# Two-layer encoder: keys and queries of the second attention group placed by DMA, and output-weight sums formed in DRAM

## The chip, the cores and the metric

The kernel runs on one core of one Trainium2 chip. TensorE (PE) multiplies matrices out of SBUF into PSUM; VectorE (DVE), ScalarE (ACT) and GpSimd (POOL) work on tiles in SBUF and PSUM, and SyncE (SP) issues most of the DMA transfers. The metric is the device time of one execution in microseconds, and a kernel's time is the median of its runs.

## What is computed

Two encoder layers over 1024 tokens of width 1024, in float32. Layer 0 runs two groups of eight attention heads side by side: group A is dense grouped-query attention, group B is latent attention, whose keys and queries are made from compressed latents. Layer 1 is windowed attention with sixteen heads. Cut to what the change touches:

```python
def mla_attention(q_lat, q_rope, c_kv, k_rope, w_uv):          # group B of layer 0
    scale = (B_NOPE + B_ROPE) ** -0.5
    sc = (einsum('bqhc,bsc->bhqs', ql, c_kv) + einsum('bqhr,bsr->bhqs', qr, k_rope)) * scale
    p = softmax(sc, axis=-1)
    o_lat = einsum('bhqs,bsc->bqhc', p, c_kv)
    return einsum('bshc,chd->bshd', o_lat, w_uv)
...
    return concatenate([oa, ob], axis=-1) @ w_out               # both layers end in a product with w_out
```

## The kernel before

**Precision.** A float32 product is made of three fast products: each operand is split into a high part (a cast by ScalarE) and a low part (the operand less its high part, by VectorE), and `mm3` (L644) adds high by high, high by low and low by high.

**Attention in layer 0.** `run_groups` (L1185) goes over 32 steps, which the code numbers 0 to 31: a step is one head and one half of the queries, 0 to 15 for group A and 16 to 31 for group B. In a step, `softmax_unit` (L1145) makes four blocks of 128 queries by 1024 keys: scores on TensorE, the row maximum on VectorE (tile nm), the exponential on ScalarE (tile Pa in group A, Pb in group B), and the division by the row sum on GpSimd. `pv_step` (L1164) takes the blocks of the step before: TensorE transposes them, ScalarE and VectorE split the transposed block (tiles hla or hlb), and TensorE multiplies it with the values.

**Scores of group B.** For head h, `qk_of` (L1432) adds three products: q1 by k1, q2 by k2 and q1 by krl. q1 and k1 hold the high parts of the 64 plain dimensions in partitions 0 to 63 and rotary parts above them. q2 and k2 hold, in two halves of 64 partitions, high and low parts in such an order that one product gives both cross terms.

**Preparing heads.** `b_heads(p, half)` (L1399) makes these tiles for heads 2p and 2p+1 and one half of the 1024 positions. One product of 128 partitions by 512 holds the keys of both heads, another their queries. The parts are taken out of PSUM 64 partitions at a time: six casts on ScalarE, four subtractions on VectorE and two copies on GpSimd (`K2E`, L1393). Rotary parts of q1 come from the scratch tensors qr_sp in DRAM, which `b_qrope` (L1342) writes. The table B_AT (L66) puts the eight calls at steps 15, 15, 19, 19, 22, 23, 27 and 27.

**Weight sums.** The two products with w_out use a scheme with fewer block products, which needs four sums of blocks of w_out for each layer and each column half. `weight_sums` (L1460) makes them ahead of time: SP loads a block into an SBUF tile, GpSimd issues transfers that add further blocks onto it, and SP stores the tile to ws_sp in DRAM after each addition. The table WS_AT (L60) puts that at steps 19 to 26. `quarter` (L1648) loads the sums later.

**What sets the order.** No engine's program is written out. All operations are recorded with their dependencies, and `Recorder.run` (L259) simulates them on a model of the engines; the times at which they start there give the order in which they are emitted. In this model an issue on SP holds it for 450 ns, and a transfer ends 500 ns after its bytes, or 3000 ns where it adds:

```python
dma_free = max(dma_free, t + 1300) + nb / (205.0 if "accum_op" in o.call[2] else 410.0)
fin = dma_free + (3000 if "accum_op" in o.call[2] else 500)
busy[e] = t + (450 if e == "SP" else o.dur)
```

On the chip each engine then works through its own program in order. All recorded operations are issued from one line, so the profile gives them L551 and tells them apart by tile.

Of the kernel before, what the change touches and what calls it, by code (L numbers as in the profile page):

```python
# [19 lines left out]
P = 128  # L20
# [38 lines left out]
W2_ENG = ("act", "dve")  # L59
WS_AT = {19: ((0, 0, False),), 20: ((0, 0, True),), 21: ((0, 1, False),), 22: ((0, 1, True),),  # L60
         23: ((1, 0, False),), 24: ((1, 0, True),), 25: ((1, 1, False),), 26: ((1, 1, True),)}
WS_SHIFT = 0
# [52 lines left out]
class Recorder:  # L115
# [143 lines left out]
    def run(self):  # L259
# [131 lines left out]
        while started < N or ev:  # L391

            for e in engs:
# [5 lines left out]
                while h:  # L399
# [12 lines left out]
                    if e == "SP" or (o.call[0].__name__ == "dma_start"):  # L412
                        nb = 4 * max(self._region(v)[2] * max(1, self._region(v)[3])
                                     for v in list(o.call[1]) + list(o.call[2].values())
                                     if isinstance(v, VP) or hasattr(v, "tensor"))
                        dma_free = max(dma_free, t + 1300) + nb / (205.0 if "accum_op" in o.call[2] else 410.0)
                        fin = dma_free + (3000 if "accum_op" in o.call[2] else 500)
                        busy[e] = t + (450 if e == "SP" else o.dur)
                    else:
                        fin = o.end  # L420
                        busy[e] = o.end
# [152 lines left out]
def encoder_kernel(ctx: ExitStack, tc: tile.TileContext, xt, ada_t, w_c1, w_c2, w_c3, w_g0, w_uq, w_ukv, w_out0, w_v1,  # L574
# [69 lines left out]
    def mm3(ps, L, R, start, stop, **kw):  # L644
        first = mm(ps, lhsT=L[0], rhs=R[0], start=start, stop=False, **kw)
        mm(ps, lhsT=L[0], rhs=R[1], start=False, stop=False, **kw)
        mm(ps, lhsT=L[1], rhs=R[0], start=False, stop=stop, **kw)
        return first

    def rstd_of(ss, n, width):  # L650
# [748 lines left out]
    def b_heads(p, half):  # L1399
# [9 lines left out]
        mm3(ps, L, R, True, True)  # L1409
        k1 = [B["k1"][e % 3], B["k1"][o % 3]]  # L1410
        nc.scalar.copy(k1[0][0:64, c], ps[0:64, :])
        nc.scalar.copy(k2[o][64:128, c], ps[64:128, :])
        nc.scalar.copy(k1[1][0:64, c], ps[64:128, :])
        K2E(k2[e][0:64, c], f(k1[0][0:64, c]))
        sub(k2[e][64:128, c], ps[0:64, :], f(k1[0][0:64, c]))
        sub(k2[o][0:64, c], ps[64:128, :], f(k2[o][64:128, c]))
        ps = PA(f"qn{p}{half}")
        for k in range(2):
            L = [a[:, p * P:(p + 1) * P] for a in B["uq"][k]]
            R = [a[:, c] for a in B["cq"][k]]  # L1420
            mm3(ps, L, R, k == 0, k == 1)
        nc.scalar.copy(q1[e][0:64, c], ps[0:64, :])
        nc.scalar.copy(q1[o][0:64, c], ps[64:128, :])
        nc.scalar.copy(q2[e][64:128, c], ps[0:64, :])
        K2E(q2[o][0:64, c], f(q1[o][0:64, c]))
        sub(q2[e][0:64, c], ps[0:64, :], f(q1[e][0:64, c]))
        sub(q2[o][64:128, c], ps[64:128, :], f(q1[o][0:64, c]))

# [27 lines left out]

    ws_sp = {(l, a, j): dr.tile([P, 1024], F32, name=f"ws{l}{a}{j}") for l in range(2) for a in range(1, 5) for j in range(2)}
    w_out = [w_out0, w_out1]

    def weight_sums(l, j, third, mark):  # L1460

        t = U(f"ws{l}{j}{int(third)}")
        w = lambda b, k: w_out[l][b, 2 * k + j]
        load(t, w(1, 0) if not third else w(0, 0), mark)
        for a, b, k in [(3, 1, 0)] if third else [(1, 1, 1), (2, 0, 0), (4, 0, 1)]:
            nc.gpsimd.dma_start(out=t, in_=w(b, k), accum_op=ALU.add)
            nc.sync.dma_start(out=ws_sp[l, a, j], in_=t)
# [586 lines left out]
```

## Time and profile before

| | us |
|---|---|
| Median of 3 runs | 1178.45 |
| Lowest and highest run | 1177.72, 1179.77 |
| The profiled execution | 1180.8 |
| Its span, from first to last instruction | 1178.1 |
| Mean granted TensorE clock, share of full speed | 0.992 |

A row of the profile reads: line, engine, operation, tile written, tile read, shapes and count; then busy time in us and mean ns of one; then the time that the engine idled just before such instructions, and what ended that. A waiting row reads: engine and its tile, what it waited for, us in total, times, longest us. A row of transfers reads: engine whose queue issued them, count, KB each, median us from issue to landing.

These slices of the span (40 equal ones, busy tenths) show where group B lies: it is worked on from about 420 to 650 us, slices 15 to 22.

```profile
PE   7999999999999999999999999999999999999996
DVE  8974889888887988888889988959776597765885
```

### The profile page before, as it was taken

To read this page: it belongs to the slowest core of one execution; us is meant where nothing else is said; L and a number is where in the kernel's file an instruction comes from. 1 tells how busy PE (TensorE), PEld (TensorE's weight loads), DVE (VectorE), ACT (ScalarE), POOL (GpSimd) and SP (SyncE) were. 2 spreads that over 40 slices of the span, in tenths; PEclk is the share of its full clock that TensorE was granted. 3 is DMA by queue.
4 is the path that set the end of the run, shared out by engine and by line. 5 is a ranking of instruction groups with operands and counts; after the bars stand their busy time and mean duration, and the time that the engine had idled before them with its cause. 6 is when DMAs were issued, how large, how long until landed. Compare 5 with 4: busy or idle time off the path is not lost.

```text
span 1178.1 us, 17460 instructions
## 1 busy us (share of the span) xinstructions
PE 1140.4 (97%) x6070; PEld 957.6 (81%) x6070; DVE 948.4 (81%) x1678; ACT 699.9 (59%) x1406; POOL 599.9 (51%) x579
## 2 busy tenths in 40 slices
PE   7999999999999999999999999999999999999996
PEld 7898877878877878788877887988888888888885
DVE  8974889888887988888889988959776597765885
ACT  5553356565555777787778832327765365565723
POOL 1334496957854645554445444704465266445414
PEclk9999999999999999999999999999999999999998
DMA  9601433232221148786125333400002212036413
GB/s 368 253 1 66 163 117 125 90 111 89 84 63 54 52 116 222 186 217 175 37 88 225 117 143 125 161 19 8 31 18 91 72 37 90 19 144 237 139 35 143
DMA packets 41671, 133.42 MB, mean 113 GB/s; under 512 B 4592, under 2 KB 9200, under 8 KB 41584
## 3 DMA queue, kind: packets, MB, share of 16 engines
q1 hardware_dynamic: 38192, 122.88, 29.4%
q0 software_dynamic: 2304, 8.39, 4.2%
q8 instruction: 47, 0.77, 0.3%
q10 hardware_dynamic: 1088, 1.05, 0.3%
q14 instruction: 40, 0.33, 0.1%
HBM read 101.24 MB, written 31.06 MB: 112 GB/s over the span
## 4 chain that ended last, share of the span: by engine, by line
PE 77%; DVE 11%; ACT 5%; DMA 3%; issue 2%; POOL 1%; SPq 0%; POOLq 0%; ACTq 0%; DVEq 0%
PE psum L551 77%; DVE nm L551 2%; DMA ada<-in_ada_t 2%; DMA w2s<-in_w_c 1%; DMA w31s<-in_w_c 1%; ACT k L551 1%; DVE hla L551 1%; ACT Pa L551 1%; ACT q L551 1%; DVE adag L551 1%; DVE xr L551 1%; ACT Pb L551 1%; DVE hl L551 1%; DVE p L551 0%; DVE hlb L551 0%
## 5 line engine op out<-in xcount | busy, mean ns | idle before, releaser
L551 DVE TENSOR_REDUCE nm<-psum 128x1 f32<-128x1024 f32 x128 | 154.6, 1217 | 16.4 <-PE psum L551 14.7
L551 POOL TENSOR_SCALAR p<-p,dn 128x384 f32<-128x384 f32 (+1 forms) x128 | 71.8, 580 | 154.9 <-ACT p L551 74.6
L551 PE MATMUL psum<-hla,VA 128*128 128x512 f32 x256 | 94.1, 427 | 9.0 <-DVE hla L551 6.5
L551 POOL TENSOR_SCALAR Pa<-Pa,rs 128x1024 f32<-128x1024 f32 x64 | 78.9, 1238 | 43.4 <-DVE rs L551 41.3
L551 POOL TENSOR_SCALAR Pb<-Pb,rs 128x1024 f32<-128x1024 f32 x64 | 72.1, 1128 | 41.6 <-DVE rs L551 39.6
L551 ACT CAST hla<-psum 128x512 fp32r<-128x512 f32 x128 | 71.3, 596 | 36.8 <-PE psum L551 30.0
L551 PE MATMUL psum<-hlb,VB 128*128 128x512 f32 x256 | 90.9, 427 | 2.2 <-DVE hlb L551 1.5
L551 DVE TENSOR_TENSOR hla<-psum,hla 128x512 fp32r<-128x512 f32 x128 | 83.8, 681 | 11.3 <-ACT hla L551 10.9
L551 ACT ACTIVATE Pa<-psum,nm 128x1024 f32<-128x1024 f32 x64 | 71.6, 1121 | 33.6 <-DVE nm L551 28.4
L551 PE MATMUL psum<-ident,Pa 128*128 128x128 f32 x512 | 89.0, 273 | 1.0 <-DVE q L551 0.8
L551 ACT ACTIVATE Pb<-psum,nm 128x1024 f32<-128x1024 f32 x64 | 71.9, 1124 | 26.8 <-DVE nm L551 24.2
L551 DVE TENSOR_TENSOR hlb<-psum,hlb 128x512 fp32r<-128x512 f32 x128 | 81.9, 683 | 7.2 <-ACT hlb L551 5.8
L551 PE MATMUL psum<-k,q 128*128 128x512 f32 x256 | 84.3, 400 | 1.0 <-ACT Pb L551 1.0
L551 DVE CUSTOM_DVE_ANT_0 p<-psum,bias,rows_g 128x384 f32<-128x384 f32 (+1 forms) x128 | 70.2, 578 | 15.4 <-PE psum L551 12.4
L551 PE MATMUL psum<-ident,Pb 128*128 128x128 f32 x512 | 79.7, 272 | 1.0 <-DVE og('0', 7)_1184 L551 0.8
L551 ACT ACTIVATE p<-p,nm 128x384 f32<-128x384 f32 (+1 forms) x128 | 74.0, 584 | 4.0 <-DVE nm L551 3.9
L551 ACT CAST hlb<-psum 128x512 fp32r<-128x512 f32 x128 | 69.2, 603 | 9.1 <-PE psum L551 7.5
L551 ACT COPY ot<-psum 64x512 f32<-64x512 f32 x64 | 37.4, 584 | 61.5 <-PE psum L551 60.8
L551 PEld LDWEIGHTS psum<-ident,Pa 128*128 128x128 f32 x512 | 64.3, 141 | 11.8 <-DVE q L551 1.0
L551 PEld LDWEIGHTS psum<-ident,Pb 128*128 128x128 f32 x512 | 63.3, 140 | 12.8 <-DVE og('0', 7)_1184 L551 1.1
L551 ACT CAST hl<-psum 128x512 fp32r<-128x512 f32 x88 | 46.2, 592 | 31.3 <-PE psum L551 29.9
L551 PEld LDWEIGHTS psum<-hla,VA 128*128 128x128 f32 x256 | 46.7, 191 | 21.8 <-DVE hla L551 10.7
(890 smaller groups left out, 3639.0 us busy)
## 6 DMA issues: line engine op xcount, KB each, us to landing
ada<-in_ada_t SPq DMA_DIRECT2D x32, 512.0 KB, 6.9
adag<-in_ada_t SPq DMA_DIRECT2D x16, 512.0 KB, 5.1
ws<-in_w_out POOLq DMA_DIRECT2D x16, 512.0 KB, 5.7
ws<-ws SPq DMA_DIRECT2D x16, 512.0 KB, 3.3
S<-ws SPq DMA_DIRECT2D x16, 512.0 KB, 4.6
o<-spill SPq DMA_DIRECT2D x12, 512.0 KB, 5.3
A<-in_w_out SPq DMA_DIRECT2D x12, 512.0 KB, 5.8
xT<-in_xt SPq DMA_DIRECT2D x8, 512.0 KB, 8.1
```

What stands on the lines that cost most here:

```text
L551: fn(*[real(v) for v in a], **{k: real(v) for k, v in kw.items()})
```

## The change

It has three parts.

1. In `b_heads`, the product in PSUM is split whole into a new SBUF tile (`two_parts`: one cast of 128 partitions, one subtraction of 128 partitions), and four transfers per product (`put`) place its 64-partition pieces into k2 or q2. These are 8 transfers of 128 KB a call and 64 in all, on SP's queue. k1 and the plain part of q1 are still cast from PSUM. The two copies on GpSimd go.
2. `weight_sums` no longer goes through SBUF. A sum is copied from DRAM to DRAM by SP and added to by transfers from DRAM to DRAM that GpSimd issues, in six steps per layer at steps 3 to 14 of the attention (group A). Copies of one sum start from another, so each step reads what the step before has left. The scratch tensors get rows of 1040 elements, of which 1024 are used.
3. In the model of the list schedule, an issue on SP holds it for 600 ns and a transfer that reads from DRAM ends 1500 ns after its bytes.

```diff
--- before.py
+++ after.py
@@ -57,8 +57,7 @@
 OLO_POOL = (((0, 0), (1, 0), (2, 0)), ((0, 0), (1, 0), (2, 0)))
 C2_EARLY = 4
 W2_ENG = ("act", "dve")
-WS_AT = {19: ((0, 0, False),), 20: ((0, 0, True),), 21: ((0, 1, False),), 22: ((0, 1, True),),
-         23: ((1, 0, False),), 24: ((1, 0, True),), 25: ((1, 1, False),), 26: ((1, 1, True),)}
+WS_AT = {3: ((0, 0),), 4: ((0, 1),), 5: ((0, 2),), 6: ((0, 3),), 7: ((0, 4),), 8: ((0, 5),),
...
 WS_SHIFT = 0
 LO_POOL = ((0, 0, 1, 0, 1), (0, 0, 0, 0, 0))
 T_POOL = (((0, 0), (0, 0), (1, 1), (1, 1)), ((0, 0), (0, 0), (1, 1), (1, 1)))
@@ -414,8 +413,9 @@
                                      for v in list(o.call[1]) + list(o.call[2].values())
                                      if isinstance(v, VP) or hasattr(v, "tensor"))
                         dma_free = max(dma_free, t + 1300) + nb / (205.0 if "accum_op" in o.call[2] else 410.0)
-                        fin = dma_free + (3000 if "accum_op" in o.call[2] else 500)
-                        busy[e] = t + (450 if e == "SP" else o.dur)
+                        src = o.call[2].get("in_")
+                        fin = dma_free + (3000 if "accum_op" in o.call[2] else 1500 if "DRAM" in str(src.space) else 500)
+                        busy[e] = t + (600 if e == "SP" else o.dur)
                     else:
                         fin = o.end
                         busy[e] = o.end
@@ -647,6 +647,16 @@
         mm(ps, lhsT=L[1], rhs=R[0], start=False, stop=stop, **kw)
         return first
 
+    def two_parts(ps, name):
+
+        t = UR(name)
+        nc.scalar.copy(t[:, 0:512], ps)
+        sub(t[:, 512:1024], ps, f(t[:, 0:512]))
+        return [[t[e * 64:(e + 1) * 64, c:c + 512] for c in (0, 512)] for e in range(2)]
+
+    def put(o, i):
+        nc.sync.dma_start(out=f(o), in_=f(i))
+
     def rstd_of(ss, n, width):
         v = SM("v")
         nc.gpsimd.tensor_scalar(v[:, :width], ss, 1.0 / n, EPS, op0=ALU.mult, op1=ALU.add)
@@ -1408,23 +1418,21 @@
         R = [a[:, c] for a in B["ckv"]]
         mm3(ps, L, R, True, True)
         k1 = [B["k1"][e % 3], B["k1"][o % 3]]
+        (he, le), (ho, lo) = two_parts(ps, f"knp{p}{half}")
         nc.scalar.copy(k1[0][0:64, c], ps[0:64, :])
-        nc.scalar.copy(k2[o][64:128, c], ps[64:128, :])
         nc.scalar.copy(k1[1][0:64, c], ps[64:128, :])
-        K2E(k2[e][0:64, c], f(k1[0][0:64, c]))
-        sub(k2[e][64:128, c], ps[0:64, :], f(k1[0][0:64, c]))
-        sub(k2[o][0:64, c], ps[64:128, :], f(k2[o][64:128, c]))
+        for d, r, x in ((k2[e], 0, he), (k2[e], 64, le), (k2[o], 64, ho), (k2[o], 0, lo)):
+            put(d[r:r + 64, c], x)
         ps = PA(f"qn{p}{half}")
         for k in range(2):
             L = [a[:, p * P:(p + 1) * P] for a in B["uq"][k]]
             R = [a[:, c] for a in B["cq"][k]]
             mm3(ps, L, R, k == 0, k == 1)
+        (he, le), (ho, lo) = two_parts(ps, f"qnp{p}{half}")
         nc.scalar.copy(q1[e][0:64, c], ps[0:64, :])
         nc.scalar.copy(q1[o][0:64, c], ps[64:128, :])
-        nc.scalar.copy(q2[e][64:128, c], ps[0:64, :])
-        K2E(q2[o][0:64, c], f(q1[o][0:64, c]))
-        sub(q2[e][0:64, c], ps[0:64, :], f(q1[e][0:64, c]))
-        sub(q2[o][64:128, c], ps[64:128, :], f(q1[o][0:64, c]))
+        for d, r, x in ((q2[e], 64, he), (q2[e], 0, le), (q2[o], 0, ho), (q2[o], 64, lo)):
+            put(d[r:r + 64, c], x)
 
     groupsB = []
     for h in range(8):
@@ -1454,23 +1462,27 @@
         return marks.get(names[n] + str(j)) if n >= 0 else None
 
 
-    ws_sp = {(l, a, j): dr.tile([P, 1024], F32, name=f"ws{l}{a}{j}") for l in range(2) for a in range(1, 5) for j in range(2)}
+    ws_sp = {(l, a, j): dr.tile([P, 1040], F32, name=f"ws{l}{a}{j}")[:, 0:1024] for l in range(2) for a in range(1, 5) for j in range(2)}
     w_out = [w_out0, w_out1]
 
-    def weight_sums(l, j, third, mark):
-
-        t = U(f"ws{l}{j}{int(third)}")
-        w = lambda b, k: w_out[l][b, 2 * k + j]
-        load(t, w(1, 0) if not third else w(0, 0), mark)
-        for a, b, k in [(3, 1, 0)] if third else [(1, 1, 1), (2, 0, 0), (4, 0, 1)]:
-            nc.gpsimd.dma_start(out=t, in_=w(b, k), accum_op=ALU.add)
-            nc.sync.dma_start(out=ws_sp[l, a, j], in_=t)
+    def weight_sums(l, step, mark):
+
+        for j in range(2):
+            S = lambda a: ws_sp[l, a, j]
+            A = lambda r, c: w_out[l][r - 1, 2 * (c - 1) + j]
+            for add, o, i in [((0, S(1), A(2, 1)), (0, S(3), A(1, 1))), ((1, S(1), A(2, 2)),),
+                              ((0, S(2), S(1)), (1, S(3), A(2, 1))), ((1, S(2), A(1, 1)),),
+                              ((0, S(4), S(2)),), ((1, S(4), A(1, 2)),)][step]:
+                if add:
+                    behind(nc.gpsimd.dma_start(out=o, in_=i, accum_op=ALU.add), mark)
+                else:
+                    load(o, i, mark)
 
     def before(n):
         m0 = mark_of(n - 1)
-        for l, j, third in WS_AT.get(n, ()):
+        for l, step in WS_AT.get(n, ()):
             with rec.at(shift=WS_SHIFT):
-                weight_sums(l, j, third, mark_of(n - 2))
+                weight_sums(l, step, mark_of(n - 1))
         with issue_after(m0), rec.at(shift=PREP_SHIFT if n else 0):
             if n == 0:
                 q_stack_a(0)
```

Since the order comes from the model, instructions move on all engines from about 115 us on. Three places follow; numbers behind names are numbers of buffers.

On VectorE, where the second pair of heads (2 and 3) is prepared, before the change. k_878 and q_877 are k2 and q2 of head 2, k_881 and q_880 those of head 3, hlb the split probabilities:

```order
L551 TENSOR_TENSOR k_878<-psum,k_678 64x512
L551 TENSOR_TENSOR k_881<-psum,k_881 64x512
L551 TENSOR_TENSOR hlb_885<-psum,hlb_885 128x512
L551 TENSOR_TENSOR q_877<-psum,q_876 64x512
L551 TENSOR_TENSOR hlb_886<-psum,hlb_886 128x512
L551 TENSOR_TENSOR q_880<-psum,q_879 64x512
L551 TENSOR_TENSOR k_878<-psum,k_678 64x512
L551 TENSOR_TENSOR hlb_887<-psum,hlb_887 128x512
L551 TENSOR_TENSOR k_881<-psum,k_881 64x512
L551 TENSOR_TENSOR hlb_888<-psum,hlb_888 128x512
L551 TENSOR_TENSOR q_877<-psum,q_876 64x512
L551 TENSOR_TENSOR q_880<-psum,q_879 64x512
```

The same place in the changed kernel, where knp and qnp are the new tiles:

```order
L551 TENSOR_TENSOR knp_885<-psum,knp_885 128x512
L551 TENSOR_TENSOR hlb_891<-psum,hlb_891 128x512
L551 TENSOR_TENSOR qnp_886<-psum,qnp_886 128x512
L551 TENSOR_TENSOR hlb_892<-psum,hlb_892 128x512
L551 TENSOR_TENSOR hlb_893<-psum,hlb_893 128x512
L551 TENSOR_TENSOR knp_887<-psum,knp_887 128x512
L551 TENSOR_TENSOR hlb_894<-psum,hlb_894 128x512
L551 TENSOR_TENSOR qnp_888<-psum,qnp_888 128x512
L551 TENSOR_TENSOR hlb_895<-psum,hlb_895 128x512
```

Eight subtractions of 64 partitions between the splits of probabilities have become four of 128.

On SP, where the first pair of heads (0 and 1) is prepared, before. q_767, q_770, q_876 and q_879 are q1 of heads 0 to 3:

```order
L551 DMA qr_sp_250<-qrh_734 128x1024
L551 DMA qr_sp_250<-qrh_736 128x1024
L551 DMA qr_sp_251<-qrl_735 128x1024
L551 DMA qr_sp_251<-qrl_737 128x1024
L551 DMA q_767<-qr_sp_250 32x1024
L551 DMA q_770<-qr_sp_250 32x1024
L551 DMA q_767<-qr_sp_251 32x1024
L551 DMA q_770<-qr_sp_251 32x1024
L551 DMA q_876<-qr_sp_250 32x1024
L551 DMA q_876<-qr_sp_251 32x1024
L551 DMA q_879<-qr_sp_250 32x1024
L551 DMA q_879<-qr_sp_251 32x1024
```

In the changed kernel (from the third row of the piece before on), with k_769, k_772 and q_768, q_771 for k2 and q2 of heads 0 and 1:

```order
L551 DMA qr_sp_251<-qrl_735 128x1024
L551 DMA qr_sp_251<-qrl_737 128x1024
L551 DMA k_772<-knp_773 64x512 x2
L551 DMA q_767<-qr_sp_250 32x1024
L551 DMA q_770<-qr_sp_250 32x1024
L551 DMA q_768<-qnp_774 64x512 x2
L551 DMA q_767<-qr_sp_251 32x1024
L551 DMA q_770<-qr_sp_251 32x1024
L551 DMA q_771<-qnp_774 64x512 x2
L551 DMA k_769<-knp_775 64x512 x2
L551 DMA k_772<-knp_775 64x512 x2
L551 DMA q_768<-qnp_776 64x512 x2
```

Loads of heads 2 and 3 have moved back, and the pieces of keys and queries stand among the loads of heads 0 and 1 and behind them.

On GpSimd, in the first group, before. Pa are probabilities that are divided, og an output that is gated, v, r and qp belong to the queries of a later pair of heads:

```order
L551 TENSOR_SCALAR Pa_384<-Pa_384,rs 128x1024
L551 TENSOR_SCALAR Pa_388<-Pa_388,rs 128x1024
L551 TENSOR_TENSOR og('0', 0)_321<-og('0', 0)_321,gT_270 64x512
L551 TENSOR_SCALAR Pa_405<-Pa_405,rs 128x1024
L551 TENSOR_SCALAR Pa_409<-Pa_409,rs 128x1024
L551 TENSOR_SCALAR v<-ssq_459 128x8
L551 TENSOR_SCALAR Pa_413<-Pa_413,rs 128x1024
L551 TENSOR_TENSOR r<-v,mhalf 128x8
L551 TENSOR_SCALAR Pa_417<-Pa_417,rs 128x1024
```

The same place in the changed kernel:

```order
L551 TENSOR_SCALAR Pa_388<-Pa_388,rs 128x1024
L551 TENSOR_TENSOR wg5l_366<-wg5s_364,wg5h_365 128x1024
L551 DMA ws_256<-in_w_out 128x1024
L551 DMA ws_257<-in_w_out 128x1024
L551 TENSOR_TENSOR og('0', 0)_321<-og('0', 0)_321,gT_270 64x512
L551 TENSOR_SCALAR Pa_405<-Pa_405,rs 128x1024
L551 TENSOR_SCALAR Pa_409<-Pa_409,rs 128x1024
L551 TENSOR_SCALAR Pa_413<-Pa_413,rs 128x1024
```

Two additions to weight sums stand between the low part of a gate's weights (wg5l) and the gated output, ahead of the next four divisions.

More of the change, by code (lines that the diff above doesn't have):

```diff
@@ L59 @@
 W2_ENG = ("act", "dve")
-WS_AT = {19: ((0, 0, False),), 20: ((0, 0, True),), 21: ((0, 1, False),), 22: ((0, 1, True),),
-         23: ((1, 0, False),), 24: ((1, 0, True),), 25: ((1, 1, False),), 26: ((1, 1, True),)}
+WS_AT = {3: ((0, 0),), 4: ((0, 1),), 5: ((0, 2),), 6: ((0, 3),), 7: ((0, 4),), 8: ((0, 5),), 9: ((1, 0),), 10: ((1, 1),), 11: ((1, 2),), 12: ((1, 3),), 13: ((1, 4),), 14: ((1, 5),)}
 WS_SHIFT = 0
```

## The prediction

> **What bounds the kernel now.** I read the page's head first, then the chain that ended last.
>
> ```profile
> span 1178.1 us, 17460 instructions
> PE 1140.4 (97%) x6070; PEld 957.6 (81%) x6070; DVE 948.4 (81%) x1678; ACT 699.9 (59%) x1406; POOL 599.9 (51%) x579
> PE 77%; DVE 11%; ACT 5%; DMA 3%; issue 2%; POOL 1%; SPq 0%; POOLq 0%; ACTq 0%; DVEq 0%
> ```
>
> TensorE is busy for 97% of the span, and the change neither adds nor removes a matmul. So it can win only what TensorE idles, 1178.1 − 1140.4 = 37.7 us over the whole span, and of that only what lies where the change works. The view of busy time by stretches says where this is (columns: length, then busy PE, PEld, DVE, ACT, POOL, granted clock, DMA share, GB/s):
>
> ```profile
> 100.00:400.00 300.00, 291.60 (x1583) 240.59 (x1581) 245.79 (x375) 170.44 (x321) 199.86 (x185) 0.99 0.28 96
> 395.00:435.00 40.00, 35.82 (x200) 28.46 (x199) 36.19 (x63) 30.22 (x59) 17.88 (x21) 1.00 0.30 93
> 435.00:470.00 35.00, 34.87 (x194) 29.17 (x193) 28.33 (x46) 24.86 (x47) 20.75 (x20) 1.00 0.74 184
> 470.00:490.00 20.00, 19.31 (x109) 15.04 (x108) 17.72 (x29) 17.15 (x32) 10.38 (x12) 1.00 0.66 181
> 490.00:520.00 30.00, 30.00 (x162) 24.81 (x161) 24.84 (x39) 22.91 (x42) 18.78 (x18) 1.00 0.85 218
> 520.00:540.00 20.00, 19.28 (x109) 15.79 (x108) 18.68 (x31) 17.59 (x34) 11.16 (x13) 1.00 0.75 181
> 540.00:590.00 50.00, 50.00 (x282) 41.96 (x281) 41.91 (x68) 35.16 (x66) 22.54 (x21) 1.00 0.33 91
> 590.00:605.00 15.00, 14.03 (x81) 10.69 (x79) 12.38 (x20) 13.97 (x27) 4.39 (x7) 1.00 0.39 141
> ```
>
> The four stretches 395, 470, 520 and 590 are those in which `b_heads` prepares a pair of the second group's heads. TensorE idles there 4.18 + 0.69 + 0.72 + 0.97 = **6.56 us**; in the three stretches between them it idles 0.13, 0 and 0. So preparing heads is what costs TensorE time in this stage. What it waited for, in the first visit (first three rows) and in the rest (last four):
>
> ```profile
> PE psum L551 <- DVE hla L551: 3.2, 4, 1.3
> PE psum L551 <- DVE q L551: 0.8, 1, 0.8
> PE psum L551 <- DVE VB L551: 0.2, 1, 0.2
> ...
> PE psum L551 <- DVE hlb L551: 1.5, 5, 0.5
> PE psum L551 <- DVE q L551: 0.5, 2, 0.2
> PE psum L551 <- ACT Pb L551: 0.2, 1, 0.2
> PE psum L551 <- ACT hlb L551: 0.2, 1, 0.2
> ```
>
> Nearly all of it is VectorE, 6.2 us of 6.6: probabilities split late (hla, hlb), because the splits of k and q stand between them on an engine that is 89 to 93% busy in the first three visits.
>
> **Part 1: splits whole, pieces placed by DMA.** These rows of 400 to 610 us price it:
>
> ```profile
> L551 DVE TENSOR_TENSOR hlb<-psum,hlb 128x512 fp32r<-128x512 f32 x96 | 61.9, 684 | 6.1 <-ACT hlb L551 4.9 <-POOL Pb L551 0.4
> L551 DVE TENSOR_TENSOR k<-psum,k 64x512 fp32r<-64x512 f32 x16 | 11.0, 689 | 5.4 <-ACT k L551 5.2
> L551 DVE TENSOR_TENSOR q<-psum,q 64x512 fp32r<-64x512 f32 x16 | 11.0, 688 | 0.6
> L551 ACT CAST hlb<-psum 128x512 fp32r<-128x512 f32 x96 | 52.0, 601 | 7.7 <-PE psum L551 6.5 <-issue 0.8
> L551 ACT CAST q<-psum 64x512 fp32r<-64x512 f32 x24 | 13.9, 581 | 0.3
> L551 POOL TENSOR_SCALAR q<-q 64x512 fp32r<-64x512 f32 x8 | 4.9, 614 | 11.4 <-ACT q L551 11.4
> ```
>
> VectorE: 32 subtractions of 64 partitions (22.0 us) become 16 of 128 partitions, and the row of hlb shows that 128 cost no more than 64: 16 × 0.684 = 10.9 us. That is 11.1 us less, 2.8 per visit. ScalarE: 48 casts of 0.581 become 32 of these and 16 of 0.601, 28.2 us for 27.9, nothing. GpSimd loses 16 copies of 0.614, 9.8 us; it waited for ScalarE ahead of them, so I count nothing.
>
> What can return to TensorE is between 0 (the freed 2.8 us per visit pass to other VectorE work) and the 6.56 us idled there. VectorE's relief per visit, 2.8, is less than the 4.18 us lost in the first and more than the 0.7 to 0.97 lost in the others. I take 2.0 of the first and 2.0 of the other three: **−4.0 us**.
>
> **Part 2: the new wait.** Scores of a head now need pieces that SP must issue and a transfer must land. The nearest rows for 128 KB, and the first visit in order of time (start, length):
>
> ```profile
> q<-qr_sp SPq DMA_DIRECT2D x16, 128.0 KB, 4.3
> kr_sp<-krraw SPq DMA_DIRECT2D x1, 128.0 KB, 1.7
> ...
> 411.63 1.65 SPq L551 DMA_DIRECT2D qr_sp<-qrl  x2
> ...
> 413.38 5.20 SPq L551 DMA_DIRECT2D q<-qr_sp  x8
> ...
> 425.02 0.50 PE L551 MATMUL psum<-k,q 128*128 128x512 f32 x1
> ```
>
> A burst goes at 5.20 / 8 = 0.65 us an issue. Today the eighth is out at 413.38 + 5.20 = 418.58 and landed by 422.9, 2.1 us before the first score at 425.02. The last store to qr_sp is out at 411.63 + 1.65 = 413.3. In the new order 12 issues stand between it and the last piece that the first score block reads (q and k, both halves of the keys): 413.3 + 12 × 0.65 = 421.1, plus 1.7 to 4.3 us gives 422.8 to 425.4. Against 425.02 that is 2.2 early to 0.4 late; if Part 1 brings the score 2 us forward, up to 2.4 late. Ends 0 and +4 (the same lateness at a fraction in the later visits, whose order leaves more matmuls between last piece and first score); nearest is the burst's own row, 4.3: **+1.0 us**. Behind a score matmul that waits stand, on TensorE, transposes and products of the group before; behind a waiting piece in SP's queue, spills and gate loads for later groups, for which TensorE waits nowhere in these stretches.
>
> The Trainium skill speaks against this: "DMA: Bandwidth & Descriptors", section "Rules for kernel authors", says of two transfers to disjoint partition halves not to bother, since both run on the same engines. By its fixed cost of about 2.0 us plus bytes over 436 GB/s ("Anatomy of one DMA") a piece would take 2.3 us, an estimate from that page; the sum would then have 0 in place of +1.0. The rows 1.7 and 4.3 lie on both sides of it.
>
> **Part 3: weight sums.** The issues change places:
>
> ```profile
> L551 POOL DMA_DIRECT2D ws<-in_w_out x16 | 14.2, 919 | 2.7 <-PE psum L551 1.6 <-DMA ws<-ws 1.1
> L551 POOL TENSOR_SCALAR Pa<-Pa,rs 128x1024 f32<-128x1024 f32 x60 | 74.3, 1245 | 34.8 <-DVE rs L551 32.6 <-PE psum L551 1.3
> ...
> POOL Pb L551 <- DVE rs L551: 38.3, 36, 5.0
> ...
> ws<-in_w_out POOLq DMA_DIRECT2D x16, 512.0 KB, 5.7
> ws<-in_w_out SPq DMA_DIRECT2D x8, 512.0 KB, 4.2
> ws<-ws SPq DMA_DIRECT2D x16, 512.0 KB, 3.3
> ```
>
> Leaving the second group frees 14.2 us of GpSimd there, but it waits 38.3 us for VectorE between 400 and 650 us, so 0. Arriving between about 150 and 360 us (the fourth to the fifteenth group) they cost 14.2 us of an engine that is 199.86 / 300 = 67% busy, mostly in pairs of 2 × 0.919 = 1.84 us, ahead of the scaling of probabilities (Pa) that TensorE transposes next. Pa has 34.8 / 60 = 0.58 us of slack each: a pair can push out 1.84 − 0.58 = 1.26 us, eight pairs 10 us at worst, 0 where the scaling is not next. TensorE's 300 − 291.6 = 8.4 us of idle between 100 and 400 ends so:
>
> ```profile
> PE psum L551 <- ACT Pa L551: 4.5, 5, 1.9
> PE psum L551 <- DVE hla L551: 3.3, 4, 1.7
> ```
>
> No GpSimd scaling is among the enders, so I stay near the low end: **+0.5 us**. A copy inside DRAM is shown by no row; its neighbours are 3.3 and 4.2 us, an accumulation 5.7, and each step stands a group behind the one that it reads, so its wait I count at nothing; late, it holds SP's queue (loads of ada and gate weights due later) and costs up to 3.
>
> **Part 4: the list's constants.** 600 for 450 and 1500 for 500 change no instruction, only the order, which is the same to about 115 us and differs on all engines from there. In the first group TensorE idles 8.4 us at places that only the order decides; that may move by ±4. I take 0.
>
> Sum: −4.0 + 1.0 + 0.5 = **−2.5 us**. Made against the profiled execution (1180.8 us, span 1178.1), 1180.8 − 2.5 = 1178.3; the runs' median lies 2.35 us below that execution, so I forecast 1178.45 − 2.5 = **1175.9 us**.
>
> **Rivals.**
> - *Hidden anyway.* VectorE's freed time goes to other work queued there, or what the splits give, the pieces' landing takes. For it: relief of 2.8 per visit against only 0.7 to 0.97 idle in three of four. Against: VectorE ended 6.2 of 6.6 us. Time 1178.
> - *Larger gain.* All 6.56 us come back, and the new order loses 1 us less in the first group: 1171.
> - *Slower, late pieces.* SP issues the pieces as slowly as the two stores above, 1.65 / 2 = 0.83 us each, and each lands after 4.3 us: the last of the 12 is out at 413.3 + 12 × 0.83 = 423.3 and landed at 427.6, 2.6 us after 425.02 and 4.6 after a score that Part 1 brought forward. It decides from 0.65 us an issue upwards. With 1 us in each later visit, less the 4.0 gained: +3.6, 1182. Against it: a piece only goes from SBUF to SBUF, and 1.7 is the shortest row of its size.
> - *Slower, accumulations in the first group.* GpSimd's work is stretched when VectorE reads SBUF twice beside it:
>
> ```profile
> 164.00 3.53 POOL L551 TENSOR_TENSOR og('0', 0)_321<-og('0', 0)_321,gT 64x512 f32<-64x512 f32 x1 [0.65 <-DVE og('0', 0)_321 L551]
> 441.25 1.28 POOL L551 TENSOR_TENSOR og('0', 3)_704<-og('0', 3)_704,gT 64x512 f32<-64x512 f32 x1 [1.64 <-DVE og('0', 3)_704 L551]
> ```
>
>   The same operation took 3.53 for 1.28 us. If half of 16 issues are stretched by 2.25 us, GpSimd loses 18 us more in its fullest stage; a third on the path is +6, with the gain 1180.5 to 1182. It decides where a pair stands right ahead of a scaling. The Trainium skill's "SBUF — State Buffer", "SBUF: two separate sides", gives this as a rule: descriptors of a DMA issued from GpSimd can't be written while VectorE holds the shared port pair.
> - *The change doesn't do what it says* (the pieces not off VectorE): excluded by the order, which has 16 fewer instructions there and 16 fewer on GpSimd.
>
> **How the numbers follow.** A measurement of this kernel tells about 0.2%, 2.4 us, from no change; the forecast is just beyond it. Chances: forecast 0.35 (its own range 1173 to 1178), larger gain 0.13, hidden 0.32, late pieces 0.11, accumulations 0.09. So faster 0.48, same 0.32, slower 0.20. The range goes from 1170 (all of the idle, and luck in Part 4) to 1182.
>
> **What would show it.** Right: VectorE's k and q rows gone, 16 rows of 0.68 us in their place; less than 4.2 us idle at the first visit, with hla and hlb as enders gone; scaling of Pa with its mean of 1245 ns. Wrong: TensorE waiting for DMA transfers into k or q, SP issues of over 0.65 us at the first visit, idle between 150 and 360 us beyond that of now, ended by a scaling.

## The result, and the profile after

| | before | after |
|---|---|---|
| Median, us | 1178.96 (1177.72 to 1179.77, 4 runs) | 1171.07 (1170.47 to 1171.49, 4 runs) |
| Ratio to before, 95% interval | | 0.9944 [0.9929, 0.9958] |
| Span of the profiled execution, us | 1178.1 | 1168.7 |
| TensorE idle, 100 to 400 us | 8.40 | 7.09 |
| TensorE idle, 395 to 605 us | 6.68 | 2.62 |

The kernel became faster by 0.56%, 6.6 us of 1179, where 2.5 us were forecast. (The ratios in this document are those on record and no quotients of the medians; the medians here lie 7.9 us apart.) The sign held, and so did the whole range of 1170 to 1182, but 1171.07 lies below the forecast's own 1173 to 1178: it is the time of the rival "larger gain" (1171). The head of the page after, and its chain that ended last:

```profile
span 1168.7 us, 17585 instructions
PE 1135.8 (97%) x6070; PEld 954.9 (82%) x6070; DVE 933.0 (80%) x1662; ACT 697.5 (60%) x1406; POOL 592.1 (51%) x563
PE 81%; DVE 7%; DMA 5%; ACT 3%; issue 1%; POOL 1%; SPq 0%; POOLq 0%; ACTq 0%; DVEq 0%
```

VectorE's share of the chain fell from 11 to 7%, and what it gave up went to TensorE. TensorE idles 1168.7 − 1135.8 = 32.9 us for 37.7, which is 4.8 us less; its busy time also fell, by 4.6 us, with the same 6070 matmuls. Most of the 4.6 us is the clock that these two executions happened to get: in the one of before, TensorE was granted half its clock for 3.4 us at 16, at 173 and at 258 us, in the one after only at 16 us, and 2 × 3.4 × 0.5 = 3.4 us of busy time go with that (last section). The view by stretches (length, busy PE, PEld, DVE, ACT, POOL, granted clock, DMA share, GB/s):

```profile
100.00:400.00 300.00, 292.91 (x1612) 241.51 (x1610) 247.71 (x386) 173.97 (x329) 213.14 (x205) 1.00 0.52 152
395.00:435.00 40.00, 38.01 (x212) 30.41 (x210) 33.88 (x59) 30.77 (x61) 15.74 (x16) 1.00 0.46 132
470.00:490.00 20.00, 19.72 (x104) 15.56 (x103) 15.41 (x24) 15.44 (x28) 5.63 (x5) 1.00 0.33 76
520.00:540.00 20.00, 20.00 (x120) 17.19 (x119) 17.49 (x31) 16.24 (x35) 7.85 (x7) 1.00 0.24 62
590.00:605.00 15.00, 14.79 (x72) 11.60 (x71) 12.74 (x19) 10.58 (x20) 5.07 (x5) 1.00 0.46 149
```

In the four visits TensorE now idles 1.99 + 0.28 + 0 + 0.21 = 2.48 us for 6.56. What it still waits for between 395 and 605 us (in total, times, longest):

```profile
PE psum L551 <- ACT Pa L551: 0.8, 1, 0.8
PE psum L551 <- DVE VB L551: 0.4, 1, 0.4
PE psum L551 <- DMA k<-knp: 0.3, 1, 0.3
PE psum L551 <- DVE hla L551: 0.2, 1, 0.2
```

Of the late splits, hlb and q are gone and hla fell from 3.2 to 0.2 us. One wait for a placed piece is there, of 0.3 us, at the first visit. The new work itself, from VectorE's groups of 400 to 610 us, GpSimd's of 100 to 400 us and the transfers:

```profile
L551 DVE TENSOR_TENSOR knp<-psum,knp 128x512 fp32r<-128x512 f32 x8 | 5.5, 684 | 2.6 <-ACT knp L551 2.6
L551 DVE TENSOR_TENSOR qnp<-psum,qnp 128x512 fp32r<-128x512 f32 x8 | 5.5, 688 | 4.5 <-ACT qnp L551 4.4
...
L551 POOL TENSOR_SCALAR Pa<-Pa,rs 128x1024 f32<-128x1024 f32 x60 | 72.0, 1216 | 29.2 <-DVE rs L551 25.0 <-PE psum L551 3.8
L551 POOL DMA_DIRECT2D ws<-in_w_out x16 | 14.4, 980 | 0.0
...
ws<-in_w_out POOLq DMA_DIRECT2D x16, 512.0 KB, 8.1
ws<-in_w_out SPq DMA_DIRECT2D x8, 512.0 KB, 8.3
ws<-ws SPq DMA_DIRECT2D x8, 512.0 KB, 5.0
k<-knp SPq DMA_DIRECT2D x32, 128.0 KB, 2.3
q<-qnp SPq DMA_DIRECT2D x32, 128.0 KB, 2.4
```

The 16 whole subtractions take 11.0 us, as forecast. The pieces land after 2.3 to 2.4 us. GpSimd's 16 issues now stand in the first group, and its scaling of Pa is no slower (1216 ns for 1245).

### The profile page after: what moved, and what is told of

Same layout as the page of the kernel before. It is cut to its first block, busy times and chain, and to the rows that moved or that the text cites. A ratio compares the mean times of both kernels' runs of the same rounds, so it can differ in the third digit from the quotient of the medians.

```text
span 1168.7 us, 17585 instructions
## 1 busy us (share of the span) xinstructions
PE 1135.8 (97%) x6070; PEld 954.9 (82%) x6070; DVE 933.0 (80%) x1662; ACT 697.5 (60%) x1406; POOL 592.1 (51%) x563
## 3 DMA queue, kind: packets, MB, share of 16 engines
q0 software_dynamic: 2304, 8.39, 4.2%
## 4 chain that ended last, share of the span: by engine, by line
PE 81%; DVE 7%; DMA 5%; ACT 3%; issue 1%; POOL 1%; SPq 0%; POOLq 0%; ACTq 0%; DVEq 0%
PE psum L551 81%; DMA ada<-in_ada_t 2%; DVE nm L551 2%; DVE p L551 1%; DMA w2s<-in_w_c 1%; DMA w31s<-in_w_c 1%; DMA o<-spill 1%; DMA xr<-in_xt 1%; ACT Pa L551 1%; DVE hla L551 1%; DVE hlb L551 1%; DVE psum L551 0%; SPq L551 0%; ACT p L551 0%; DVE hT10l L551 0%
## 5 line engine op out<-in xcount | busy, mean ns | idle before, releaser
L551 DVE TENSOR_REDUCE nm<-psum 128x1 f32<-128x1024 f32 x128 | 154.4, 1216 | 17.2 <-PE psum L551 15.7
L551 POOL TENSOR_SCALAR Pa<-Pa,rs 128x1024 f32<-128x1024 f32 x64 | 76.4, 1210 | 42.7 <-DVE rs L551 29.2
L551 DVE TENSOR_TENSOR hl<-psum,hl 128x512 fp32r<-128x512 f32 x88 | 55.6, 684 | 10.5 <-ACT hl L551 10.1
```

What stands on the lines that cost most here:

```text
L551: fn(*[real(v) for v in a], **{k: real(v) for k, v in kw.items()})
```

## The experiments

Each kernel was timed beside the kernel before on the same chip, whose median was 1177.94, 1177.83, 1178.35 and 1177.39 us in the four sets. Idle is TensorE's, in us, in two stretches of the profiled execution. It belongs to one execution: five kernels with one and the same order of TensorE up to about 400 us (before, e1_place, f1_halves, f2_twice, f4_late) idle 7.27 to 9.13 us between 100 and 400 us.

| Kernel | Median, us | Ratio to before | Idle 100–400 | Idle 395–605 |
|---|---|---|---|---|
| before | | 1 | 8.40 | 6.68 |
| e1_place | 1172.06 | 0.9957 [0.9943, 0.9971] | 7.27 | 3.66 |
| e2_sums | 1174.92 | 0.9973 [0.9963, 0.9984] | 6.40 | 6.56 |
| e3_const | 1178.92 | 1.0001 [0.9991, 1.0012] | 7.13 | 6.64 |
| e4_place_sums | 1169.78 | 0.9925 [0.9911, 0.9939] | 6.38 | 2.92 |
| f1_halves | 1180.31 | 1.0020 [1.0008, 1.0032] | 7.41 | 9.80 |
| f2_twice | 1186.62 | 1.0078 [1.0066, 1.0091] | 9.13 | 10.84 |
| f3_shift | 1178.27 | 1.0007 [0.9994, 1.0019] | 8.39 | 8.69 |
| f4_late | 1177.04 | 0.9998 [0.9988, 1.0009] | 8.26 | 6.58 |
| g1_load | 1177.51 | 0.9995 [0.9987, 1.0004] | 6.43 | 6.58 |
| g2_issues | 1181.22 | 1.0033 [1.0021, 1.0045] | 6.38 | 11.95 |
| g3_copies | 1169.94 | 0.9931 [0.9919, 0.9943] | 6.22 | 2.23 |
| h1_changed | 1171.43 | 0.9949 [0.9933, 0.9966] | 7.22 | 3.24 |

Counting matmuls compares executions better than windows of time do, since the first 2100 matmuls, the first 2600 and the first 3500 are the same ones in all kernels of the next table. The first count is reached just ahead of the first visit, the second between the second and the third, the third behind the fourth. Times are in us, from the traces.

| Kernel | start to the 2100th | 2100th to the 2600th | 2600th to the 3500th |
|---|---|---|---|
| before | 402.0 | 98.6 | 166.7 |
| after | 397.6 | 95.2 | 163.9 |
| e1_place | 399.1 | 96.1 | 163.9 |
| e2_sums | 396.8 | 98.8 | 166.6 |
| e4_place_sums | 396.6 | 95.4 | 164.0 |
| f1_halves | 399.0 | 96.2 | 173.9 |
| f3_shift | 398.9 | 101.5 | 166.8 |
| f4_late | 401.6 | 98.7 | 166.8 |
| g1_load | 397.0 | 98.6 | 168.5 |

### The parts of the change, one by one

**e1_place** has Part 1 and its transfers (Part 2) alone; weight sums and constants are those of before.

```diff
 WS_AT = {19: ((0, 0, False),), 20: ((0, 0, True),), ...
+        (he, le), (ho, lo) = two_parts(ps, f"knp{p}{half}")
+            put(d[r:r + 64, c], x)
```

> Only the pieces of keys and queries are placed by DMA; weight sums and constants as before. The order of all engines is that of before until the first pair of heads is prepared, so TensorE's idle time between 100 and 390 us must stay within 0.5 us of the 8.4 of before. My theory (relief of VectorE at the four visits, as the prediction has it): idle at the four visits falls from 6.6 to about 2.5 us or less, time 1174 to 1176 (ratio 0.996 to 0.998). Rival A (the gain of the whole change in the second group is due to the weight sums leaving it): ratio 0.999 to 1.001. Rival B (late pieces): TensorE waits for transfers into k or q, ratio over 1.000.

**e2_sums** has the weight sums alone.

```diff
+WS_AT = {3: ((0, 0),), 4: ((0, 1),), ...
+    def weight_sums(l, step, mark):
```

> Only the weight sums are moved to the first group and into DRAM. My theory (GpSimd waited for VectorE in the second group, so it wins nothing there; in the first group the issues cost 0 to 0.5 us): ratio 0.999 to 1.001. Rival A (the sums leaving the second group is what helps there): idle at the four visits falls below 4 us, ratio 0.995 to 0.998. Rival C (two issues in a row hold up the division of probabilities): idle between 150 and 360 us grows by 1 us or more, ended by GpSimd, ratio over 1.001.

**e3_const** has the two constants alone.

```diff
+                        fin = dma_free + (3000 if "accum_op" in o.call[2] else 1500 if "DRAM" in str(src.space) else 500)
+                        busy[e] = t + (600 if e == "SP" else o.dur)
```

> Only the two constants of the list schedule are changed; every instruction is that of before, in another order. The changed kernel lost some 4.5 us less than before in the first group, where my prediction had nothing to gain. Rival D (a truer model of loads orders the first group better): idle plus slow restarts in the first group falls by 3 us or more, ratio 0.995 to 0.998. My theory (an order without direction): ratio anywhere within 0.998 to 1.002, and the first group no better than by 1.5 us.

**e4_place_sums** has the first two together, with the constants of before.

> Pieces placed by DMA and weight sums moved, constants as before. If the constants are what helps (rival D), this stays 3 us or more behind the changed kernel: ratio 0.996 to 0.999. If they do nothing, it is the changed kernel's 0.994 within 0.001. If the parts add up, its gain is the sum of those of placing and of sums alone, within 0.001.

The placing gains 0.43% of 1177.94 = 5.1 us, the weight sums 0.27% = 3.2 us, both 0.75% = 8.8 us: they add up within the intervals. The constants alone do nothing. The two gains lie in different places: e1_place brings the idle of 395 to 605 us from 6.68 to 3.66, while e2_sums leaves it (6.56) and lowers that of 100 to 400 us. The counts agree: the four visits, from the 2100th matmul to the 3500th, take 265.3 us before, 260.0 in e1_place and 265.4 in e2_sums. Four expectations did not hold. The visits of e1_place idle 3.65 us and not 2.5. It idles 7.1 us from 100 to 390 us, 1.3 less than before, although TensorE's order is that of before up to 402 us. None of the three readings set out for e2_sums foresaw a gain in the first group. And e4_place_sums lies 0.002 below the changed kernel, although the constants alone do nothing (see h1_changed). e2_sums also shows that GpSimd's freed time in the second group is worth nothing there: the enders of its waits between 390 and 640 us are still VectorE's.

```profile
PE psum L550 <- DVE hla L550: 3.2, 4, 1.3
PE psum L550 <- DVE hlb L550: 1.4, 5, 0.5
PE psum L550 <- DVE q L550: 1.2, 3, 0.8
```

### Where the weight sums' gain comes from

**f4_late** has the sums from DRAM to DRAM but at steps of the second group, where the order of TensorE, ScalarE and VectorE is that of the kernel before, row by row. **f3_shift** has them in the first group, one step later than e2_sums.

```diff
-WS_AT = {3: ((0, 0),), 4: ((0, 1),), ...
+WS_AT = {17: ((0, 0),), 18: ((0, 1),), ...     # f4_late
+WS_AT = {4: ((0, 0),), 5: ((0, 1),), ...       # f3_shift
```

> The weight sums from DRAM to DRAM, but kept in the second group (steps 17 to 28). TensorE, ScalarE and VectorE run the very order of the kernel before; only GpSimd's issues and SP's queue differ. Theory (the gain of e2_sums comes from the order in the first group): ratio 0.999 to 1.001, idle in the four stretches as before (6.2 to 6.6 us). Rival (DRAM to DRAM as such gains): 0.997 to 0.998. A third (the longer copies and accumulations cost when they stand beside the visits): 1.001 to 1.003, with SP's loads or GpSimd's scalings late there.

> The weight sums alone (e2_sums), each step one group later (4 to 15 for 3 to 14): the same copies and accumulations, the same GpSimd load in the first group, but another order of TensorE's work there. Theory (the gain of 3.2 us in e2_sums is the luck of one order in the first group): the ratio moves away from 0.9973, to anywhere between 0.997 and 1.003, and the difference to before again arises at places in the first group, 100 to 400 us. Rival (the gain belongs to the sums as such, no store of a sum from SBUF or fewer bytes through it): 0.9973 within 0.001.

f4_late gives 0.9998: DRAM to DRAM gains nothing as such, and its slower transfers cost nothing beside the visits. f3_shift gives 1.0007: the same transfers one step later gain nothing on the whole. Not all of that lies in the first group: its order also lengthens the first visit, where it takes 101.5 us from the 2100th to the 2600th matmul for 98.6, while its first group, at 398.9 us, ends between that of before and that of e2_sums. The 3.2 us of e2_sums are a property of the order that its table happened to give TensorE in the first group. In the order of before, TensorE has three waits of 1.83, 1.70 and 1.95 us there, at 170, 196 and 255 us; in that of e2_sums it has one of that size, and all waits between 100 and 390 us come to 6.1 us:

```profile
PE psum L550 <- ACT Pa L550: 5.1, 8, 1.8
PE psum L550 <- DVE hla L550: 0.8, 2, 0.6
PE psum L550 <- DVE cqT L550: 0.2, 1, 0.2
```

Its idle of 100 to 400 us is 8.40 − 6.40 = 2.0 us less. Much of the rest is probably the clock behind such waits, in the last section.

### Whether the placing's gain is VectorE's relief

**f1_halves** is e1_place with the old number of subtractions; the scheduler was free to choose an order for it.

```diff
-        sub(t[:, 512:1024], ps, f(t[:, 0:512]))
+        for r in (0, 64):
+            sub(t[r:r + 64, 512:1024], ps[r:r + 64, :], f(t[r:r + 64, 0:512]))
```

> The placing alone (e1_place), but VectorE subtracts each split in two halves of 64 partitions, 32 subtractions of about 0.69 us as in the kernel before, and not 16 of 128 partitions. ScalarE's whole cast, the 64 transfers and GpSimd's missing copies stay. Theory (the gain of the placing is VectorE's relief of 2.8 us per visit): the relief is gone, TensorE's idle in the four stretches goes back to 5 to 6.5 us with probabilities split late (hla, hlb) as enders, and the ratio to before is 0.999 to 1.001 (e1_place: 0.9957). Rival (the gain comes from GpSimd's 16 copies that went, or from the changed order of the visits): the ratio stays at 0.995 to 0.997.

The gain is gone (1.0020), but the profile doesn't show the reason that was expected. The largest wait is another: at 554 us TensorE waits 4.99 us for a scaling of Pb. The timeline, in order of time (start, length, engine, operation, count, and in brackets the idle before it and what ended that):

```profile
550.33 7.84 SPq L551 DMA_DIRECT2D ws<-ws  x2
552.23 0.88 POOL L551 DMA_DIRECT2D ws<-in_w_out  x1 [5.33 <-DMA ws<-ws]
552.85 2.52 POOL L551 TENSOR_SCALAR Pb<-Pb,rs 128x1024 f32<-128x1024 f32 x2
554.33 0.47 PE L551 MATMUL psum<-ident,Pb 128*128 128x128 f32 x1 [4.99 <-POOL Pb L551]
```

GpSimd stood 5.33 us before an accumulation of the old weight sums, whose SBUF tile was still being stored, and the scaling behind it in its queue came late. That comes from the old sums and not from the halves, so the ratio of f1_halves doesn't settle the question.

Its first two visits, which lie ahead of this wait, say something all the same. Here are the stretches of e1_place and then of f1_halves:

```profile
395.00:435.00 40.00, 37.47 (x207) 30.24 (x206) 33.69 (x59) 30.18 (x59) 17.55 (x18) 1.00 0.51 147
470.00:490.00 20.00, 19.13 (x104) 14.90 (x103) 15.89 (x24) 16.22 (x30) 5.30 (x6) 1.00 0.97 248
```

```profile
395.00:435.00 40.00, 37.88 (x208) 30.23 (x206) 36.60 (x63) 29.97 (x58) 15.09 (x16) 1.00 0.52 145
470.00:490.00 20.00, 19.71 (x110) 16.20 (x109) 18.29 (x29) 16.31 (x32) 6.15 (x7) 1.00 0.88 234
```

VectorE is as busy in f1_halves as before the change (36.60 of 40 us, 18.29 of 20), and still TensorE idles only 2.12 + 0.29 us, where it idled 4.18 + 0.69. From the 2100th to the 2600th matmul f1_halves takes 96.2 us, e1_place 96.1, before 98.6. So in these two visits the gain is there without the relief, in an order that the scheduler made for the old load. In the last two it seems not to be, as an estimate: 173.9 us less the wait of 4.99 and less 5.8 × 0.5 = 2.9 for the half clock behind it (to 560.1 us) is 166.0, before 166.7, e1_place 163.9.

**g1_load** puts the old VectorE load into e4_place_sums with the order held fixed: the scheduler sees one subtraction, and two of 64 partitions are emitted in its place.

```diff
-        sub(t[:, 512:1024], ps, f(t[:, 0:512]))
+        lo = nc.vector.tensor_tensor(out=t[:, 512:1024], in0=ps, in1=f(t[:, 0:512]), op=ALU.subtract)
+        lo.cut = [(slice(r, r + 64),) for r in (0, 64)]
...
+                for s in o.cut or (None,):
+                    fn(*a, **{k: v[s] if s and hasattr(v, "tensor") else v for k, v in kw.items()})
```

> Placing and weight sums (e4_place_sums) in exactly its order on every engine, but each of the 16 whole subtractions is issued as two of 64 partitions, one right behind the other: VectorE does 32 of about 0.69 us as in the kernel before, 11 us more than e4_place_sums in the four visits. Nothing else differs. Theory A (the gain of the placing is VectorE's relief, 2.8 us per visit): the gain of the placing, 5 us, is lost, ratio to before 0.996 to 0.998 (e4_place_sums: 0.9925), and hla or hlb of VectorE end TensorE's waits in the four stretches again, for 3 us more. Theory B (f1_halves had the old VectorE load, yet idled only 2.1 us in the first stretch: the gain comes from what the splits no longer wait for, and from the order around them, and f1_halves lost its gain to one wait for a GpSimd accumulation of the old weight sums): ratio 0.992 to 0.9945, idle in the four stretches within 1.5 us of e4_place_sums.

The ratio goes from 0.9925 to 0.9995: 11 us of VectorE work in the visits cost 0.70%, 8.2 us. This is theory A, and more than its 0.996 to 0.998, and more than the 5.1 us that the placing gained: probably because the fixed order was made for the lighter engine, so that the old load hurts more in it than it did in the kernel before (its visits take 267.1 us, those of before 265.3). So g1_load shows that this order needs VectorE's lighter load. It doesn't show that the placing gains by nothing else: another order kept the gain of the first two visits with the old load. The enders of 395 to 605 us are the expected ones:

```profile
PE psum L556 <- DVE hlb L556: 2.6, 8, 0.5
PE psum L556 <- DVE hla L556: 1.9, 4, 0.9
PE psum L556 <- ACT Pa L556: 0.5, 1, 0.5
PE psum L556 <- DVE VB L556: 0.4, 1, 0.4
```

In e4_place_sums the same stretch has four waits and none for hlb; here there are fourteen. Idle there grows by 3.66 us only, but TensorE's busy time grows too, from 1134.5 to 1139.4 us over the span, at the same granted clock of 0.996 and with the same matmuls.

**g3_copies** puts the load back on GpSimd in place of VectorE: 16 of the pieces are GpSimd copies again, in e4_place_sums' order.

```diff
-    def put(o, i):
-        nc.sync.dma_start(out=f(o), in_=f(i))
+    def put(o, i, pool=False):
+        d = nc.sync.dma_start(out=f(o), in_=f(i))
+        if pool:
+            d.other = lambda o_, i_: rec.nc.gpsimd.tensor_scalar(o, f(i), 1.0, 0.0, op0=ALU.mult, op1=ALU.add)
```

> Placing and weight sums (e4_place_sums) in its order, but 16 of the 64 pieces are put in place by GpSimd copies of 64 x 512 (0.61 us each, as many as the kernel before had) and not by transfers. Theory (GpSimd's copies that went are worth nothing, it waited for others there): ratio 0.992 to 0.994, as e4_place_sums. Rival (they are part of the gain: GpSimd's scalings of Pa and Pb in the visits come later by 0.6 us each): TensorE waits for scalings of Pa or Pb (ended by POOL, or by ACT behind them) 1 to 3 us more in the four stretches, ratio 0.995 or above.

0.9931 lies within the interval of e4_place_sums, and idle in 395 to 605 us is 2.23 us. In this order GpSimd's 16 copies, together with 16 issues fewer on SP, are worth nothing in either direction.

### How near the placed pieces are to being late

**f2_twice** is e1_place with each piece in two transfers of half the columns; **g2_issues** is the same on e4_place_sums, emitted in its fixed order.

```diff
-        nc.sync.dma_start(out=f(o), in_=f(i))
+        for x in (0, 256):
+            nc.sync.dma_start(out=f(o[:, x:x + 256]), in_=f(i[:, x:x + 256]))   # f2_twice
...
+        d = nc.sync.dma_start(out=f(o), in_=f(i))                               # g2_issues
+        d.cut = [(slice(None), slice(x, x + 256)) for x in (0, 256)]
```

> The placing alone (e1_place), with each piece sent in two transfers of 256 columns: 128 transfers of 64 KB for 64 of 128 KB, so 16 issues more on SP in each visit, some 10 us of its time. If the pieces have slack (theory: no wait for them was seen in e1_place, about 2 us ahead of the first scores): the ratio is that of e1_place, 0.9957, within 0.0015, and TensorE waits for a transfer into k or q for under 1 us. Rival (the pieces land only just in time, the new wait is near): TensorE waits for pieces in each visit, 1 to 3 us each, and the ratio is 0.999 to 1.005.

> Placing and weight sums (e4_place_sums) in exactly its order, but each piece goes as two transfers of 256 columns issued one behind the other: 128 of 64 KB for 64 of 128 KB, the same bytes. In f2_twice this cost 1.2%, with the scheduler free to choose another order and the old weight sums' stores in SP's queue. Theory (pieces are near their limit: issues on SP, 0.6 us each, not bytes set when they land): TensorE waits for pieces (k, q) 3 us or more, ratio 0.996 or above. Rival (the stores of the old weight sums and the new order made f2_twice late): TensorE waits under 1 us for pieces, ratio 0.992 to 0.994.

Twice the issues for the same bytes cost 0.9925 → 1.0033, 12.7 us, with the order fixed, and 0.9957 → 1.0078 with a free one. That is worse than f2_twice's rival, which allowed up to 1.005; TensorE waits there 5.2 us for pieces of keys and 0.9 for pieces of queries. The waits of g2_issues between 390 and 640 us:

```profile
PE psum L556 <- DMA q<-qr_sp: 6.8, 1, 6.8
PE psum L556 <- DMA k<-knp: 3.3, 2, 1.9
```

The longest is for a rotary part that SP issues behind the pieces. SP's queue at that place, in e4_place_sums and then in g2_issues:

```profile
413.01 1.19 SPq L550 DMA_DIRECT2D k<-knp  x2
414.26 1.03 SPq L550 DMA_DIRECT2D q<-qr_sp  x2
```

```profile
417.98 2.46 SPq L556 DMA_DIRECT2D k<-knp  x4
420.48 1.04 SPq L556 DMA_DIRECT2D q<-qr_sp  x2
```

A transfer of 64 KB holds SP for 2.46 / 4 = 0.62 us, one of 128 KB for 1.19 / 2 = 0.60: an issue of half the bytes costs the same. The rotary part goes out 6.2 us later, and TensorE waits 6.8 us for it. So the changed kernel stands close to the limit of SP's queue at the first visit; its own 0.3 us wait there is the first sign.

### The constants beside the other parts

**h1_changed** is the changed kernel itself, to set it beside e4_place_sums, which lacks only the constants.

> The changed kernel itself, all three parts, with more runs than the first measurement had (0.9944, four runs). Theory (the constants cost something together with the other two parts, since they choose another order of the first group): 0.994 to 0.996, apart from e4_place_sums (0.9925, without them). Rival (they are worth nothing here too): 0.992 to 0.9935.

Its 0.9949 and the first 0.9944 stand above e4_place_sums (0.9925) and g3_copies (0.9931). The constants probably cost about 2 us there, but the intervals still touch. Part of it is seen in the profile: idle of 100 to 400 us is 7.09 and 7.22 us with them and 6.38 without. e4_place_sums has the lowest ratio of all that were run.

## Why the prediction was right in sign and too small

- **What bounds the kernel.** That preparing heads cost TensorE its time in the second group was read rightly. But "it can win only what TensorE idles" was too narrow. Span fell by 9.4 us between the two profiles, of which 4.6 us is shorter busy time. Some 3.4 of these are the clock of the two executions, so the profiles overstate what the change did, but waits can cost clock too. And in g1_load idle and busy time grow together (3.66 us in the stretch, 4.9 over the span) at the same clock. A matmul behind a wait has none before it to overlap with, which is a likely reason; it was not tested by itself.
- **Part 1, −4.0.** Right in place and nearly in size. With the new transfers it measured −5.1 us where the two parts together were put at −3.0, and it lies at the visits, as forecast. The mechanism is shown in part. In the order of e4_place_sums VectorE's load decides: g1_load adds the old load alone and loses more than the gain. But the reason given, that splits of probabilities come late because VectorE is 89 to 93% busy, is not enough: in f1_halves it is 91% busy in the first two visits (36.60 of 40 us, 18.29 of 20), and TensorE loses no more than in e1_place. How the 5.1 us divide between the lighter load and the order around the whole splits stays open. "Hidden anyway" was wrong: the visits gained. GpSimd's zero held in g3_copies; ScalarE's was not tested alone.
- **Part 2, +1.0.** Too large. The row of 4.3 us was chosen as the nearest for the landing; the pieces took 2.3 to 2.4 us, nearer to the lower row of 1.7. The forecast's estimate of 2.3 us, from the Trainium skill's "DMA: Bandwidth & Descriptors" ("Anatomy of one DMA"), agrees with the trace, although that section gives its formula for transfers issued from GpSimd and SP issued these. The issue rate held at the first visit, 0.56 to 0.66 us an issue in most rows. What remains is one wait of 0.3 us. The rival "late pieces" was wrong for this kernel but right in kind: it decides by SP's issues, and g2_issues brought it about.
- **Part 3, +0.5.** The step that failed, and the largest error of the sum: measured alone it was −3.2 us. The forecast counted the load of 16 issues on GpSimd and looked for a scaling behind them; their mean of 0.98 us was near the forecast's 0.92, no scaling became slower, and no cost appeared. That they would move the whole first group into another order, and remove two of three long waits, was granted only to Part 4, as ±4 with a middle of 0. f3_shift and f4_late show that this gain hangs on the table's exact steps. No row that the forecast read gives its sign, so that it came out as a gain is luck; its size lies within the ±4. Against 3.7 us here, Parts 1 and 2 together were 2.1 off (−5.1 for −3.0). The rival "larger gain" hit the time by another sum: it had all 6.56 us of the visits and 1 us of the first group, where idle fell by 4.1 and 1.3 us.
- **The accumulations rival** is refuted: with 16 of them in the first group, an issue took 0.98 us for 0.92, and not 2.25 more, and the scaling of Pa 1216 ns for 1245.
- **Part 4, 0.** Right alone (1.0001). Together with the others the constants probably cost 2 us, within its ±4.

## What to carry to other kernels

Moving work off the engine that ends the waits paid here, even at the price of 16 transfers a visit; check the issuing queue first, since halving the bytes of a transfer did not shorten its issue. When a list scheduler rebuilds the order, one kernel with an edit tells little of the edit: hold the order fixed and change only what is emitted, or move the edit by one step and see whether the gain stays.

## What the runs showed of the hardware that was not expected

**A wait of under 2 us can halve TensorE's clock, in some executions and not in others.** This is the kernel before, behind its wait of 1.83 us that ends at 171.46 us (granted clock third from the end); in all, about 3.4 us there are granted half the clock:

```profile
173.00:176.00 3.00, 3.00 (x9) 2.25 (x8) 1.58 (x3) 1.08 (x3) 3.00 (x4) 0.50 0.00 0
```

e4_place_sums and g3_copies run the same order in the first group. At 171 us both wait 1.83 us for Pa. The stretch 165 to 185 us of e4_place_sums, then of g3_copies:

```profile
165.00:185.00 20.00, 18.01 (x103) 14.67 (x102) 17.28 (x28) 13.57 (x25) 19.47 (x23) 1.00 0.52 195
```

```profile
165.00:185.00 20.00, 18.02 (x97) 14.67 (x96) 15.88 (x26) 12.37 (x24) 18.02 (x21) 0.91 0.52 194
```

The idle is the same, 2.0 us, but six matmuls fewer fit into it. In the 6 us behind this wait the mean granted clock is 1.00 in six of the eleven traces with it and 0.72 in the other five (before, e1_place, f2_twice, f4_late, g3_copies), about (1 − 0.72) × 6 = 1.7 us lost. Behind the wait of 1.95 us at 255 us it is 0.72 in four traces of six, behind that of 1.70 us 1.00 in all six. This gives an estimate for e2_sums: its order lacks the wait of 1.95 us, so it gains 2.0 us of idle and 4/6 × 1.7 = 1.1 us of clock, 3.1 where 3.2 were measured. It is a rough one: the five traces in the order of before reach the 2100th matmul after 399.0 to 404.2 us, the five in that of e2_sums after 396.6 to 398.3. f3_shift lacks that wait too; what its first group saved went at the first visit. Behind the wait of 4.99 us in f1_halves, 554 to 558 us was granted half the clock:

```profile
554.00:558.00 4.00, 3.67 (x9) 2.92 (x10) 0.00 (x0) 0.00 (x0) 1.36 (x2) 0.50 0.74 134
```

The Trainium skill's "TensorE: Matmul & The Clock Gate" ("Why this matters for your kernels") advises against idle gaps of over about 3 us, and ("What's actually happening") has the activity window run free of the kernel. The second agrees with a wait that halves the clock in about half of the traces; for the first the traces decide, and 1.83 us is enough.

**Transfers from DRAM to DRAM took longer than those of the same size from DRAM into SBUF**: 8.3 us for 4.2 for a copy of 512 KB of w_out, 8.1 for 5.7 for an accumulation, medians from issue to landing. Part of that is the place: in f4_late, where they stand in the second group as before, it was 7.4 and 6.3. TensorE, VectorE and ScalarE waited for none of them in the profile after; SP's queue stood 28.7 us for accumulations to land (77.9 before).
